# The seventh operand of a Strassen feed-forward, made before the stage instead of inside its first job

## The chip, the cores and the metric

The kernel runs on one core of one Trainium2 chip. The metric is the device time of one execution in microseconds (us), the median of several runs. Engines are named as the profile names them: PE (TensorE), PEld (its weight loads), DVE (VectorE), ACT (ScalarE), POOL (GpSimd) and SP (SyncE, which here only issues DMAs).

## What is computed

One layer of a hybrid encoder on 1024 positions of width 1024: a gated token mixer (a convolution module beside a bidirectional gated recurrence, the "scan"), its output projection, and a convolutional gated feed-forward with 2816 hidden columns. The part around the change is:

```python
x = x + jnp.einsum("bsd,de->bse", y, w_out[layer])
h2 = _rmsnorm(x, ffn_norm_w[layer])
up = jnp.einsum("bsd,df->bsf", h2, w_up)            # 1024 x 1024 times 1024 x 5632
gate, val = jnp.split(up, 2, axis=-1)
gate = _dwconv_centred(gate, dw_w, dw_b)            # three taps along the positions
x = x + jnp.einsum("bsf,fd->bsd", jax.nn.silu(gate) * val, w_down)
```

## The kernel before

**Layout.** Activations are held transposed, 128 channels by 512 positions a tile (2 KB in each partition), so 1024 x 1024 values are eight row groups by two halves. Every product is taken with split operands: `split` (L120) makes a high part by a cast on ACT (L121) and a low part by a subtraction on DVE (L118), and `mm3` (L138 to L145) issues three matmuls of 512 columns, high by high, high by low, low by high. The first of the three needs only the casts, the second the low part of the activations, the third the low part of the weights.

**The order.** PE executes its instructions in the order of the program text (L87). The other engines' queues are ordered by a planner, which walks the program with modelled durations before anything runs; on the chip each queue then executes in that fixed order, and an instruction that waits holds everything behind it on its engine.

**Memory pools.** A pool opened after another was released takes over its bytes. Its pages are held back one by one, each by the last use of the old pages that lie under it (`reuse_waits="tile"`). After the scan, its pool `hp` is released (L1058) and two are opened: `fw` (L1061), which lives to the end of the feed-forward's first half, and `p4` (L1062), which holds the merged activations `mg` and the tiles `x2` and `xq` for the output projection. After `p4.release()` (L1136), `fu` (L1139) takes over its bytes.

**The stages around the change.**
1. The last head of the scan and the last jobs of the projection `w_in` (`dense`), then the jobs with `hgrn_o_w` (L1083 to L1085). Their operand `bm` is loaded from DRAM into `tm` pages, split into `hx` pages (`bm_loads`, L1002), and merged with the gates by `merge` (L1065).
2. The jobs with `w_out` (L1118 to L1125). `x2_evac` (L1091) adds the input, stores `x2`, squares it for the norm and makes the scaled tile `xq`, stored as `d_h2` (`d_h` in the profile). After every second job the loop at L1126 to L1135 makes four operands of the next stage from the tiles still on the chip: numbers 1, 2, 6 and 5, each 4 row groups of a high and a low `hx` page.
3. The feed-forward's first half: 22 jobs `ffn_job(0..21)`, each a 2 x 2 block product by Strassen's scheme in Winograd's form, seven products (`pair_job`, L224) in the order 1, 2, 6, 7, 5, 4, 3, of 4 x 3 matmuls each. Below, "P7" is product 7, and "P7 of job 0" that of the first job.
4. `w_down` and the final norm.

**The weights of a job** (`prep`, L232): `rows` (a page of `wr`, two of them) and `col` (`sw`, a single page) are loaded by SP (L243, L244), `a22` (`w4`, a single page) too (L246). POOL issues three accumulating DMAs (`add`, L238): one adds to `col`, then one adds half of `col` to `rows`, then one adds the two halves of `rows`. Before, between and after these, five casts and subtractions make the split pages: w1 and w2 and later w6 and w3 in pages `wp` (four, in the pool `mp` that is always there); w7 and w5 from `col`, and w4 from `a22`, in pages `wq` (three). `wq`, `sw` and `w4` lie in the pool called `wpool`, which is `fw` for the feed-forward. A single `sw` page means that the next job's `col` is loaded when this job's w7 and w5 are split and its second `add` has landed. `run_jobs` (L149) prepares the next job four steps into the present one, that is after its second product.

**The operands 7, 4 and 3** are made from copies in DRAM after the first two products of job 0 have been issued (L1201 to L1219): `late_load` brings tiles back into `ft` pages (four of them, in `fu`). Operand 7 takes two loads, a subtraction (L1211) and a split for each of 4 row groups; operand 4 one load, two additions (L1216) and a split; operand 3 one load and a split. The results lie in 24 `hy` pages of `fu`. Between P1 and P2 stand 16 small matmuls for the norm (L420), and between P2 and P6 the matmuls that spread its result over the partitions (L412, fed by eight activations at L411).

Of the kernel before, what the change touches and what calls it, by code (L numbers as in the profile page):

```python
# [10 lines left out]
F32 = mybir.dt.float32  # L11
F32R = mybir.dt.float32r
# [3 lines left out]
ALU = mybir.AluOpType  # L16
AX = mybir.AxisListType

P = 128
# [25 lines left out]
def tile_hybrid_encoder(  # L45
# [24 lines left out]
    V, A, G, T = nc.vector, nc.scalar, nc.gpsimd, nc.tensor  # L70
# [20 lines left out]
    def nm(s):  # L91
        uid[0] += 1
        return f"{s}_{uid[0]}"
# [3 lines left out]
    def bank(tag):  # L97
        return ps.tile([P, H], F32, tag=tag, name=nm(tag), bufs=BANKS[tag])

    def page(pool, tag, bufs, dt=F32):  # L100
        return pool.tile([P, H], dt, tag=tag, name=nm(tag), bufs=bufs)

    def tmp():
        return page(mp, "tm", 4)
# [4 lines left out]
    def hx():  # L109
        return page(mp, "hx", 32, F32R)  # L110
# [6 lines left out]
    def split_lo(eng, lo, src, hi):  # L117
        eng.tensor_tensor(lo, src, hi.bitcast(F32), op=ALU.subtract)  # L118

    def split(hi, lo, src, eng):  # L120
        A.copy(hi, src)  # L121
        split_lo(eng, lo, src, hi)
        return hi, lo
# [4 lines left out]
    def raw_w(src, nk):  # L128
        t = mp.tile([P, nk, P], F32, tag="wr", name=nm("wr"), bufs=2)
        nc.sync.dma_start(t, src)  # L130
        return t

    def w_page(nk, pool=None):
        if pool is None:
            return mp.tile([P, nk, P], F32R, tag="wp", name=nm("wp"), bufs=4)
        return pool.tile([P, nk, P], F32R, tag="wq", name=nm("wq"), bufs=3)

    def mm3(acc, w, act, k, first, last, again=False):  # L138


        whi, wlo = w
        ahi, alo = act
        T.matmul(acc, whi[:, k, :], ahi, start=first, stop=False, skip_group_check=again)  # L143
        T.matmul(acc, whi[:, k, :], alo, start=False, stop=False, skip_group_check=again)  # L144
        T.matmul(acc, wlo[:, k, :], ahi, start=False, stop=last, skip_group_check=again)  # L145
# [78 lines left out]
    def pair_job(src0, src1, nk, acts, wpool, pool, evac, su=4):  # L224

        def prep():  # L232
            def both(src, alt):
                hi, lo = split(w_page(2 * nk, alt), w_page(2 * nk, alt), src, V)
                return [(hi[:, :nk], lo[:, :nk]), (hi[:, nk:], lo[:, nk:])]

            def add(o, a):
                G.dma_start(o, a, accum_op=ALU.add)  # L238

            w = {}  # L240
            rows = raw_w(src0, 2 * nk)
            col = wpool.tile([P, 2 * nk, P], F32, tag="sw", name=nm("sw"), bufs=1)
            nc.sync.dma_start(col[:, :nk], src0[:, :nk])  # L243
            nc.sync.dma_start(col[:, nk:], src1[:, :nk])  # L244
            a22 = wpool.tile([P, nk, P], F32, tag="w4", name=nm("w4"), bufs=1)
            nc.sync.dma_start(a22, src1[:, nk:])  # L246
            add(col, src1)
            w[1], w[2] = both(rows, None)
            add(rows[:, :nk], col[:, nk:])
            w[7], w[5] = both(col, wpool)  # L250
            add(rows[:, nk:], rows[:, :nk])
            w[6], w[3] = both(rows, None)
            one = w_page(2 * nk, wpool)
            w[4] = split(one[:, :nk], one[:, nk:], a22, V)
            return w

        def run(w):
            def product(i, acc, first=True):
                for k in range(nk):
                    mm3(acc, w[i], acts(i)[k], k, first and k == 0, k == nk - 1, not first)  # L260
                    if k % 2 == 1 or k == nk - 1:
                        yield

            def copy(acc):
                t = page(pool, "su", su)
                A.copy(t, acc)  # L266
                return t

            row, b2, col = bank("mm"), bank("tr"), bank("sc")
            yield from product(1, row)  # L270
            p1 = copy(row)
            yield from product(2, b2)
            evac(0, 0, b2, p1, ALU.add)
            yield from product(6, row, False)
            u2 = copy(row)
            yield from product(7, col)
            p7 = copy(col)
            yield from product(5, row, False)
            evac(1, 1, p7, row, ALU.subtract)
            yield from product(4, col, False)  # L280
            evac(1, 0, col, u2, ALU.subtract)
            yield from product(3, row, False)
            evac(0, 1, row)

        return prep, run

    def combos(ops, k, b11, b12, b22, alloc):
# [111 lines left out]
    NK2 = ND // 2  # L399
# [128 lines left out]
    for k in range(NK2):  # L528
        b21 = page(p1, "su", 4)
# [133 lines left out]
    for half in range(2):  # L663
        xs = []
        for j in range(NCW):
            if j % 2 == 0:
                both = p1.tile([P, 2, H], F32, tag="ca", name=nm("cx"), bufs=2)
# [16 lines left out]
        for j, xn in enumerate(xs):  # L684
# [3 lines left out]
            both = gp0.tile([P, 2, H], F32R, tag="gl", name=nm("ch"), bufs=NCW)  # L688
# [322 lines left out]
    for h in range(NH):  # L1011
# [4 lines left out]
        for half in range(2):  # L1016
            i = 2 * h + half
# [43 lines left out]
    fw = tc.alloc_tile_pool(name="fw", bufs=1, reuse_waits="tile")  # L1061
# [25 lines left out]
    h2 = {i: [] for i in range(1, 8)}  # L1087
# [23 lines left out]
        return evac  # L1111

    h2_pages = {i: [(hx(), hx()) for _ in range(NK2)] for i in (1, 2, 6, 5)}

    def parts(i, k, src):
        h2[i].append(split(*h2_pages[i][k], src, V))
# [9 lines left out]
    for k in range(NK2):  # L1126
        s_out.fill(16 if k else 17) if k < NK2 - 1 else s_out.drain()
        b11, b12, b21, b22 = x2[k][0], x2[k][1], x2[k + NK2][0], x2[k + NK2][1]
        t5, t6 = tmp(), tmp()
        parts(1, k, b11)  # L1130
        V.tensor_tensor(t5, b11, b12, op=ALU.subtract)
        parts(2, k, b21)
        V.scalar_tensor_tensor(t6, t5, -1.0, b22, op0=ALU.mult, op1=ALU.subtract)
        parts(6, k, t6)
        parts(5, k, t5)  # L1135
    p4.release()  # L1136

# [1 line left out]
    fu = tc.alloc_tile_pool(name="fu", bufs=1, reuse_waits="tile")  # L1139
# [59 lines left out]
    rstd2 = [next(st) for st in stats]  # L1199

    def late_parts(i, src):  # L1201
        h2[i].append(split(page(fu, "hy", 24, F32R), page(fu, "hy", 24, F32R), src, V))

    def late_load(kk, half):
        t = page(fu, "ft", 4)
        nc.sync.dma_start(t, d_h2[kk][half])
        return t

    for k in range(NK2):
        b12, b22 = late_load(k, 1), late_load(k + NK2, 1)  # L1210
        V.tensor_tensor(b12, b12, b22, op=ALU.subtract)  # L1211
        late_parts(7, b12)
    for k in range(NK2):
        b21 = late_load(k + NK2, 0)
        for part in h2[6][k]:
            V.tensor_tensor(b21, b21, part.bitcast(F32), op=ALU.add)  # L1216
        late_parts(4, b21)
    for k in range(NK2):
        late_parts(3, late_load(k + NK2, 1))  # L1219
# [152 lines left out]
```

## Time and profile before

| What | us |
|---|---|
| median of 3 runs | 1898.19 (1895.85 to 1900.01) |
| the profiled execution | 1905.6 |
| its span (first to last instruction) | 1903.8 |
| `w_out` jobs on PE, from 1099.8 to 1186.8 | 87.0 |
| first job of the feed-forward, from 1186.83 to 1226.18 | 39.35 |
| a later job, from 1245.80 to 1265.20 | 19.40 |

Times inside the execution are us from the start of the span. The profile's parts used below are its page (totals, the chain of work that ended last), the timeline of an engine (start, duration, engine, line, operation, out<-in, count, and in brackets the idle time before and what ended it), the busy time of the engines by stretches, groups of instructions, and DMA issues with their time to landing. "PEclk" is the share of its clock that PE was granted.

### The profile page before, as it was taken

To read this page: it belongs to the slowest core of one execution; us is meant where nothing else is said; L and a number is where in the kernel's file an instruction comes from. 1 tells how busy PE (TensorE), PEld (TensorE's weight loads), DVE (VectorE), ACT (ScalarE), POOL (GpSimd) and SP (SyncE) were. 2 spreads that over 40 slices of the span, in tenths; PEclk is the share of its full clock that TensorE was granted. 3 is DMA by queue.
4 is the path that set the end of the run, shared out by engine and by line. 5 is a ranking of instruction groups with operands and counts; after the bars stand their busy time and mean duration, and the time that the engine had idled before them with its cause. 6 is when DMAs were issued, how large, how long until landed. Compare 5 with 4: busy or idle time off the path is not lost.

```text
span 1903.8 us, 23750 instructions
## 1 busy us (share of the span) xinstructions
PE 1799.7 (95%) x8543; PEld 1484.0 (78%) x8543; DVE 1270.2 (67%) x1860; ACT 799.2 (42%) x1488; POOL 210.9 (11%) x218
## 2 busy tenths in 40 slices
PE   6988999999999998999998999899999999999996
PEld 5767878887778887888786888588888888788885
DVE  3488999535469898999835555667676666534445
ACT  6433333234554554555443134544343344522124
POOL 3101111213100001000100000111111111000000
PEclk9999999999999999999998999899999999999998
DMA  7747788786563333342237665777676676733134
GB/s 256 219 119 169 179 188 199 185 182 148 190 192 89 113 108 96 111 122 82 75 95 216 197 200 183 185 153 154 147 151 143 143 156 128 221 93 96 54 89 162
DMA packets 323916, 285.09 MB, mean 150 GB/s; under 512 B 14926, under 2 KB 245078, under 8 KB 323798
## 3 DMA queue, kind: packets, MB, share of 16 engines
q1 hardware_dynamic: 272006, 242.67, 41.5%
q0 software_dynamic: 51792, 40.90, 15.2%
q8 instruction: 67, 1.10, 0.3%
q14 instruction: 51, 0.42, 0.1%
HBM read 191.24 MB, written 71.83 MB: 138 GB/s over the span
## 4 chain that ended last, share of the span: by engine, by line
PE 66%; DVE 13%; DMA 8%; ACT 6%; issue 3%; POOL 2%; SPq 0%; ACTq 0%; POOLq 0%; DVEq 0%
PE mm L143 16%; PE mm L144 16%; PE mm L145 16%; PE sc L144 3%; PE sc L145 3%; PE sc L143 3%; PE tr L143 2%; PE tr L144 2%; PE tr L145 2%; DVE wp L118 1%; DVE kG L730 1%; DVE DE L730 1%; PE sc L838 1%; DVE qF L730 1%; DMA wr<-wr 1%
## 5 line engine op out<-in xcount | busy, mean ns | idle before, releaser
L143 PE MATMUL mm<-hx,wp 128*128 128x512 f32 x1176 | 482.6, 410 | 24.6 <-ACT hx L121 8.6
L145 PE MATMUL mm<-hx,wp 128*128 128x512 f32 x1176 | 467.4, 397 | 3.9 <-DVE wp L118 3.9
L144 PE MATMUL mm<-hx,wp 128*128 128x512 f32 x1176 | 466.8, 397 | 2.9 <-POOL hx L118 1.9
L121 ACT CAST wp<-wr 128x1024 fp32r<-128x1024 f32 (+2 forms) x196 | 179.7, 917 | 323.0 <-PE mm L144 222.9
L143 PEld LDWEIGHTS mm<-hx,wp 128*128 128x128 f32 x1176 | 226.5, 193 | 73.7 <-ACT hx L121 9.5
L118 DVE TENSOR_TENSOR wp<-wr,wp 128x1024 fp32r<-128x1024 f32 (+2 forms) x196 | 206.9, 1056 | 102.9 <-ACT wp L121 97.4
L145 PEld LDWEIGHTS mm<-hx,wp 128*128 128x128 f32 x1176 | 225.5, 192 | 55.1 <-DVE wp L118 5.4
L144 PEld LDWEIGHTS mm<-hx,wp 128*128 128x128 f32 x1176 | 226.5, 193 | 48.4 <-POOL hx L118 3.6
L645 DVE SCALAR_TENSOR_TENSOR acc<-gl,v_b,acc 128x1024 f32<-128x1024 f32 x120 | 150.1, 1285 | 0.5
L143 PE MATMUL sc<-hy,wq 128*128 128x512 f32 x244 | 97.3, 399 | 3.1 <-ACT hy L121 3.0
L144 PE MATMUL sc<-hy,wq 128*128 128x512 f32 x244 | 96.7, 396 | 2.7 <-DVE hy L118 2.7
L145 PE MATMUL sc<-hy,wq 128*128 128x512 f32 x244 | 96.2, 394 | 0.0
L238 POOL DMA_DIRECT2D wr<-sw x39 | 34.9, 896 | 519.3 <-DVE wp L118 297.4
L1251 DVE TENSOR_TENSOR xr<-mm,xr 128x512 f32<-128x512 f32 x48 | 33.1, 690 | 82.0 <-PE mm L145 82.0
L838 PEld LDWEIGHTS sc<-qF,A 128*128 128x128 f32 x512 | 65.9, 193 | 19.0 <-issue 13.3
L838 PE MATMUL sc<-qF,A 128*128 128x128 f32 x512 | 69.1, 278 | 11.7 <-DVE qF L730 10.6
L121 ACT CAST wq<-sw 128x1024 fp32r<-128x1024 f32 x39 | 41.1, 1054 | 86.6 <-PE mm L144 66.4
L143 PE MATMUL mm<-hy,wp 128*128 128x512 f32 x156 | 63.2, 405 | 7.4 <-ACT wp L121 5.3
L266 ACT COPY su<-mm 128x512 f32<-128x512 f32 x78 | 45.5, 583 | 53.4 <-PE mm L145 53.4
L835 ACT COPY A<-kG 128x512 f32<-128x512 f32 x64 | 39.7, 620 | 66.3 <-DVE kG L730 37.8
L1169 DVE SCALAR_TENSOR_TENSOR tm<-gp,v_a,tm 128x512 f32<-128x512 f32 x88 | 65.6, 746 | 1.8 <-ACT tm L1165 0.9
L1153 DVE TENSOR_TENSOR ft<-su,mm 128x512 f32<-128x512 f32 x22 | 15.1, 687 | 71.6 <-issue 68.1
(281 smaller groups left out, 3548.6 us busy)
## 6 DMA issues: line engine op xcount, KB each, us to landing
wr<-in_w_in_dram SPq DMA_DIRECT2D x55, 512.0 KB, 6.5
sw<-in_ffn_w_up_dram SPq DMA_DIRECT2D x44, 256.0 KB, 3.5
sw<-in_ffn_w_up_dram POOLq DMA_DIRECT2D x22, 512.0 KB, 8.3
wr<-in_ffn_w_up_dram SPq DMA_DIRECT2D x22, 512.0 KB
d_g<-ft SPq DMA_DIRECT2D x44, 256.0 KB, 5.9
ev<-d_g SPq DMA_DIRECT2D x44, 256.0 KB, 3.2
wr<-sw POOLq DMA_DIRECT2D x39, 256.0 KB, 3.3
wr<-wr POOLq DMA_DIRECT2D x39, 256.0 KB, 3.8
```

The source lines that it names most:

```text
L118: eng.tensor_tensor(lo, src, hi.bitcast(F32), op=ALU.subtract)
L121: A.copy(hi, src)
L143: T.matmul(acc, whi[:, k, :], ahi, start=first, stop=False, skip_group_check=again)
L144: T.matmul(acc, whi[:, k, :], alo, start=False, stop=False, skip_group_check=again)
L145: T.matmul(acc, wlo[:, k, :], ahi, start=False, stop=last, skip_group_check=again)
L238: G.dma_start(o, a, accum_op=ALU.add)
L266: A.copy(t, acc)
L645: V.scalar_tensor_tensor(acc, g[:, k : k + S], tap(k), acc, op0=ALU.mult, op1=ALU.add)
L730: V.tensor_tensor(o, a, b, op=op)
L835: A.copy(A_t.rearrange("p (b x e) -> p b x e", x=2, e=h), pairs(kG, h))
L838: T.matmul(b[:, c * P : (c + 1) * P].rearrange("p (b x e) -> p b x e", x=2, e=h), A_t[:, c * P : (c + 1) * P], view(qF, c * P, [[2 * h, P ...
L1169: V.scalar_tensor_tensor(c, g[:, o + k : o + k + H], vec("fdw", k * NF + j), c, op0=ALU.mult, op1=ALU.add,)
```

## The change

- Operand 7 is made in the loop at L1126 from the tiles still on the chip, with 1, 2, 6 and 5, into eight pages `h7` of a tag of its own in `fw`. Its difference t7 is taken first, t6 follows from t7 and t5 is taken last, so that the loop uses three temporary pages for each row group instead of two.
- The late loop for operand 7 (eight loads, four subtractions, four splits) is gone, and `hy` has 16 pages instead of 24.
- The pages `w4` and `wq` move from `wpool` to `pool`: for the feed-forward, from `fw` to `fu`. (For the jobs with `w_in`, which use the same function, both names mean one pool, and nothing moves.) `sw` stays in `fw`.

```diff
             col = wpool.tile([P, 2 * nk, P], F32, tag="sw", name=nm("sw"), bufs=1)
...
-            a22 = wpool.tile([P, nk, P], F32, tag="w4", name=nm("w4"), bufs=1)
+            a22 = pool.tile([P, nk, P], F32, tag="w4", name=nm("w4"), bufs=1)
...
-            w[7], w[5] = both(col, wpool)
+            w[7], w[5] = both(col, pool)
...
-            one = w_page(2 * nk, wpool)
+            one = w_page(2 * nk, pool)
...
     h2_pages = {i: [(hx(), hx()) for _ in range(NK2)] for i in (1, 2, 6, 5)}
+    h2_pages[7] = [[page(fw, "h7", 2 * NK2, F32R) for _ in range(2)] for _ in range(NK2)]
...
-        t5, t6 = tmp(), tmp()
+        t7, t6, t5 = tmp(), tmp(), tmp()
         parts(1, k, b11)
+        V.tensor_tensor(t7, b12, b22, op=ALU.subtract)
+        parts(2, k, b21)
+        V.tensor_tensor(t6, t7, b11, op=ALU.subtract)
+        parts(6, k, t6)
+        parts(7, k, t7)
         V.tensor_tensor(t5, b11, b12, op=ALU.subtract)
-        parts(2, k, b21)
-        V.scalar_tensor_tensor(t6, t5, -1.0, b22, op0=ALU.mult, op1=ALU.subtract)
-        parts(6, k, t6)
         parts(5, k, t5)
...
-        h2[i].append(split(page(fu, "hy", 24, F32R), page(fu, "hy", 24, F32R), src, V))
+        h2[i].append(split(page(fu, "hy", 16, F32R), page(fu, "hy", 16, F32R), src, V))
...
-    for k in range(NK2):
-        b12, b22 = late_load(k, 1), late_load(k + NK2, 1)
-        V.tensor_tensor(b12, b12, b22, op=ALU.subtract)
-        late_parts(7, b12)
```

## The prediction

> **What bounds the kernel now.** First the page: who is busy, and who stands on the chain that ended last.
>
> ```profile
> PE 1799.7 (95%) x8543; PEld 1484.0 (78%) x8543; DVE 1270.2 (67%) x1860; ACT 799.2 (42%) x1488; POOL 210.9 (11%) x218
> PE 66%; DVE 13%; DMA 8%; ACT 6%; issue 3%; POOL 2%; SPq 0%; ACTq 0%; POOLq 0%; DVEq 0%
> ```
>
> PE sets the time. A change that removes no matmul can gain only where PE stands still or runs slowly. So second, the busy times by stretches around the touched code:
>
> ```profile
> core 0: us, PE busy (x) PEld busy (x) DVE busy (x) ACT busy (x) POOL busy (x), PEclk, DMA share, GB/s
> 1002.57:1018.87 16.30, 7.04 (x17) 5.07 (x17) 8.15 (x12) 7.54 (x12) 0.00 (x0) 0.58 0.59 185
> 1199.40:1226.18 26.78, 19.83 (x50) 12.08 (x50) 19.94 (x30) 10.64 (x18) 3.40 (x3) 0.70 0.60 167
> 1245.80:1265.20 19.40, 19.40 (x86) 15.91 (x85) 12.69 (x17) 8.24 (x12) 3.33 (x3) 1.00 0.77 163
> 1099.80:1186.80 87.00, 87.00 (x385) 72.06 (x384) 45.41 (x63) 35.96 (x54) 1.73 (x2) 1.00 0.62 192
> ```
>
> In the `w_out` stage (last row) and in a later feed-forward job PE has no gap: nothing is to be had there, and work added there on DVE (45.41 of 87.00 us busy) is covered. 384 matmuls in 87.00 us give the full rate, 0.2266 us each. The two upper rows are the holes. The lower hole is where operands 7, 4 and 3 are made; PE's timeline:
>
> ```profile
> 1199.17 0.39 PE L145 MATMUL mm<-hx,wp 128*128 128x512 f32 x1
> ...
> 1200.05 0.49 PE L143 MATMUL sc<-hy,wq 128*128 128x512 f32 x1 [0.49 <-ACT hy L121]
> 1201.74 0.51 PE L144 MATMUL sc<-hy,wq 128*128 128x512 f32 x1 [1.20 <-DVE hy L118]
> ...
> 1220.92 0.76 PE L143 MATMUL mm<-hy,wp 128*128 128x512 f32 x1 [1.17 <-ACT hy L121]
> ...
> 1226.18 0.63 PE L143 MATMUL mm<-hx,wp 128*128 128x512 f32 x1
> ```
>
> P6 of job 0 ends at 1199.40 (one issue interval after the first row), job 1 begins at 1226.18. P7, P5, P4 and P3 are 48 matmuls, 10.9 us at the full rate, and take 26.78: **15.9 us too much**, in waits for `hy` and in matmuls at a clock of 0.70. What `hy` waits for, in the chain of work in order of time:
>
> ```profile
> 1192.66 6.56 DMA ft<-d_h
> ...
> 1201.72 3.08 DMA ft<-d_h
> ...
> 1205.61 3.24 DMA ft<-d_h
> ```
>
> It is the reloading of operand 7's tiles through four `ft` pages.
>
> The upper hole is at the end of the scan, 190 us ahead of the feed-forward. PE, then ACT, then the chain:
>
> ```profile
> 1002.34 0.39 PE L145 MATMUL mm<-hx,wp 128*128 128x512 f32 x1
> 1011.00 0.79 PE L143 MATMUL mm<-hx,wp 128*128 128x512 f32 x1 [8.27 <-ACT hx L121]
> 1012.79 0.80 PE L144 MATMUL mm<-hx,wp 128*128 128x512 f32 x1 [1.00 <-DVE hx L118]
> ```
>
> ```profile
> 998.05 0.62 ACT L121 CAST hx<-tm 128x512 fp32r<-128x512 f32 x1 [2.61 <-DMA tm<-d_bm]
> 998.92 0.63 ACT L121 CAST hx<-tm 128x512 fp32r<-128x512 f32 x1 [0.25 <-DMA tm<-d_bm]
> 1007.43 1.04 ACT L121 CAST wq<-sw 128x1024 fp32r<-128x1024 f32 x1 [7.88 <-DMA sw<-in_ffn_w_up_dram]
> 1008.39 0.61 ACT L121 CAST wq<-w 128x512 fp32r<-128x512 f32 x1
> 1008.91 1.04 ACT L121 CAST wp<-wr 128x1024 fp32r<-128x1024 f32 x1
> ...
> 1010.34 1.65 ACT L121 CAST hx<-tm 128x512 fp32r<-128x512 f32 x3
> ```
>
> ```profile
> 996.66 10.75 DMA sw<-in_ffn_w_up_dram
> ```
>
> PE waits for `bm`'s fifth row group. Its cast stands on ACT behind the casts of w7/w5 and w4 of feed-forward job 0, and these wait for the accumulating DMA into `sw`, which lands at 1007.41. The planner put them there because `wq` lies in `fw`, which opens after the scan. From 1002.57 to 1018.87 PE issues 15 matmuls, 3.4 us at the full rate: **12.9 us too much**.
>
> **The change part by part.** *wq and w4 to `fu`.* Their pages now lie under `mg`, which is read to the end of `w_out`. So the two casts and two subtractions cannot stand at 1007 any more, nor the `a22` loads at SP's head:
>
> ```profile
> 993.97 0.92 SPq L114 DMA_DIRECT2D tm<-d_bm  x2
> ...
> 999.42 2.05 SPq L114 DMA_DIRECT2D tm<-d_bm  x3
> 1010.37 0.38 SPq L246 DMA_DIRECT2D w<-in_ffn_w_up_dram  x1
> ```
>
> What is late next is `bm` itself. The two loads issued from 993.97 released casts at 998.05 and 998.92, some 4.2 us each; the three issued from 999.42 share the engines with the accumulate, so I take landings of 1005, 1006 and 1007 (bounds: 1003.6 by 4.2 us, 1007.4 when the accumulate is over). A cast (0.62) and PE resumes at 1005.7; the last group's low part is there at 1008.6, and the four groups are through at about 1009.9 instead of 1005.3: 4.6 us stay. Before, the clock was 0.58 in that stretch, and 12.9 less the two waits of PE (8.27 and 1.00) leaves 3.6 us to it. A gap of 3.1 us may do it too: 0 to 4 us, I take 2. So 6.6 of 12.9 stay, **6.3 gained** (3 to 8.3).
> The Trainium skill ("TensorE: Matmul & The Clock Gate", section "What's actually happening") says that the clock halves after an idle window of about 3.4 us and returns after a busy one, and that the windows run freely; it speaks against a full gain, since 3.1 us is under it by little. By it alone the term would be 0 or about 1.7 us (half of 3.4, an estimate); the trace agrees that the clock is halved after 8.27 us, and no row shows a gap of 3.1.
>
> *Operand 7 from tiles on the chip.* Gone: eight loads of 256 KB, four subtractions at L1211, four casts and four low parts. Added in the loop: for each row group one subtraction (t7), one cast, one low part. Prices:
>
> ```profile
> L118 DVE TENSOR_TENSOR hy<-ft,hy 128x512 fp32r<-128x512 f32 x12 | 8.1, 687 | 1.9 <-ACT hy L121 1.8
> L1216 DVE TENSOR_TENSOR ft<-ft,hx 128x512 f32<-128x512 f32 x8 | 5.2, 686 | 1.3 <-DMA ft<-d_h 1.3
> L1211 DVE TENSOR_TENSOR ft<-ft,ft 128x512 f32<-128x512 f32 x4 | 2.8, 690 | 5.3 <-DMA ft<-d_h 5.3
> ```
>
> That is 1.4 us of DVE and 0.62 of ACT a row group. Three of the four lie under `w_out`, where DVE has 41 us to spare; without that cover they would cost 4. The third `tm` page delays nothing there: a job takes PE 10.9 us. The fourth group comes after `w_out`, with the casts that moved (1.05 and 0.62 on ACT, 1.22 and 0.69 on DVE). Behind them stand the norm's activations, for which P6 waits; ACT and DVE have gaps there, so I take 0.7 (0 to 5: the rival below).
>
> Then P7 and P5 follow P6 at once, and P4 is wanted at 1204.8, P3 at 1207.6. DVE can begin the eight additions and four low parts of operand 4 when the first four late loads land, 1198 as before, and needs 8.2 us for them (0.69 each) and some 1.7 for what stands between: P4 is late by 0 to 2, I take 0.5. Operand 3 gets its `ft` pages one by one from operand 4, each load 3.1 us (second and third row of the chain above), a cast and a low part: its last group stands at about 1212, wanted at 1209.9, 2.2 us.
>
> Last, the weights of job 1. `sw` is reloaded when w7/w5 of job 0 are split, now at about 1192.5 instead of 1182:
>
> ```profile
> 1188.00 1.57 POOL L238 DMA_DIRECT2D sw<-in_ffn_w_up_dram  x1 [4.95 <-DMA sw<-in_ffn_w_up_dram]
> ...
> 1201.38 0.95 POOL L238 DMA_DIRECT2D wr<-sw  x1 [7.75 <-DVE wp L118]
> 1206.37 0.87 POOL L238 DMA_DIRECT2D wr<-wr  x1 [4.04 <-DMA wr<-sw]
> ```
>
> ```profile
> sw<-in_ffn_w_up_dram POOLq DMA_DIRECT2D x2, 512.0 KB, 7.7
> ...
> sw<-in_ffn_w_up_dram SPq DMA_DIRECT2D x2, 256.0 KB, 4.3
> ...
> wr<-sw POOLq DMA_DIRECT2D x1, 256.0 KB, 4.7
> wr<-wr POOLq DMA_DIRECT2D x1, 256.0 KB, 4.8
> ```
>
> 4.3 + 7.7 + 4.7 + 4.8 us, a cast of 1.05 and 1 for issues make 23.6: w6 of job 1 stands at 1216, wanted by its P6 at 1212.5 + 5.4 = 1218. It fits by 2 us; I take 1 (0 to 5) for what the loads do to each other, and 1 (0 to 4) for a clock that falls in these waits. Later jobs have the cover of the gapless row above. Together 5.4 of 15.9 stay, **10.5 gained** (5 to 14.4).
> The Trainium skill ("DMA: Bandwidth & Descriptors", section "Issuing engines are not separate DMA queues") says that DMAs from all queues interleave on the same 16 engines, which speaks against moving `a22` and `sw` to 1190; it names no price, and by it the 1 us becomes the 5 of my range.
>
> **The sum.** 6.3 + 10.5 = 16.8 us off the span of 1903.8: 1887.0. The profiled execution (1905.6) is 7.4 above the median, so the difference is taken from the median: 1898.19 - 16.8 = **1881.4**.
>
> **The rivals.**
> - *Only the feed-forward gains.* `bm` lands late anyway, or another cast with a wait takes the head of ACT at 1000. For: the accumulate still runs there. Against: `bm`'s casts at 1010.34 waited for no DMA. 1898.2 - 10.5 = 1887.7.
> - *Only the scan's end gains.* `a22` is loaded at 1190, lands after 6.6 us as `ft` did, and its cast on ACT holds the norm's activations: P6 5 us later, and 3.6 us of slow clock as at the scan's end. The second gain falls to 10.5 - 8.6 = 1.9: 1898.2 - 8.2 = 1890.0.
> - *Slower: the reload of `sw`.* If SP has it behind the late loads, as job 2's reload was before (row below), it goes out at about 1217, w6 of job 1 stands at 1240.6, and PE waits 22.6 us from 1218 and loses 3.6 to the clock: 4.4 + 22.6 + 3.6 = 30.6 instead of the 15.9 lost there before, less the 6.3 gained: 8.4 us slower, 1906.6. Each us of the reload is one of the time; it decides from 1208.5. Against: eight late loads are half of sixteen, and the planner let a ready `sw` load go first at 1181.97.
>
> ```profile
> 1181.97 0.38 SPq L243 DMA_DIRECT2D sw<-in_ffn_w_up_dram  x1
> ...
> 1218.40 0.38 SPq L243 DMA_DIRECT2D sw<-in_ffn_w_up_dram  x1
> ```
>
> - *It does nothing:* the planner, which orders everything anew, makes waits elsewhere (at the end of the feed-forward's first half, say) that eat the gain: 1898.
>
> **Chances.** Forecast 0.60 (gains of 3 + 5 to 8.3 + 14.4: 1875.5 to 1890), feed-forward only 0.12, scan only 0.11, slower 0.09, nothing 0.08. Range 1874 to 1893: it leaves out the last two and the edges of the others. A measurement of this kernel tells about 0.2%, 3.8 us. Faster 0.83, same 0.08, slower 0.09.
>
> **What would show it.** No `wq` cast near 1007, and a gap of PE there of 2 to 4 us. No L1211; P7 right behind P6; gaps at P4 and P3 under 3 us; the reload of `sw` before 1195 and no wait of PE for `wp` in job 1. Wrong would be a gap of over 5 us between P2 and P6, a `sw` reload after 1205, or a hole that stays at 1002 to 1011.

## The result, and the profile after

The median after is 1890.92 us (9 runs, 1886.05 to 1897.06); before, on the same chip, 1900.52 us (9 runs). The ratio is 0.9955 (95% interval 0.9938 to 0.9972): 8.6 us faster (5.3 to 11.8), where 16.8 were forecast. The time, 1890.92, lies inside the forecast's range and 9.5 us above its point. Three more comparisons of the same kernel gave 0.9947, 0.9939 and 0.9950 (intervals with the experiments); over all of them the medians are 1890.4 us (39 runs) and 1900.7 us (87 runs), so the gain is some 10 us.

The profiled execution of after took 1889.98 us, with a span of 1888.2. From its page, totals by engine: PE has the same 8543 instructions as before and is busy 9.3 us less; most of that is in P7 to P3, where its busy time fell from 19.83 to 11.10 us and PEclk rose from 0.70 to 1.00.

```profile
PE 1790.4 (95%) x8543; PEld 1477.7 (78%) x8543; DVE 1270.7 (67%) x1860; ACT 797.8 (42%) x1488; POOL 212.4 (11%) x218
```

Now the stretches, cut at the same matmuls in each kernel. Busy time of the engines, PEclk, DMA share and GB/s, first two stretches of before that the prediction did not show (from the last four matmuls of P2 to the end of P6 of job 0, called "P2 to P6" below; job 1), then four of after (the scan's end; P2 to P6; P7 to P3; job 1):

```profile
1193.20:1199.40 6.20, 5.93 (x21) 3.42 (x19) 2.04 (x4) 4.46 (x12) 0.44 (x5) 1.00 1.03 288
1226.18:1245.80 19.62, 19.62 (x85) 16.05 (x84) 12.87 (x17) 9.32 (x12) 1.75 (x2) 0.98 0.72 160
```

```profile
1001.07:1008.96 7.89, 5.73 (x17) 3.74 (x16) 3.37 (x5) 2.99 (x5) 0.00 (x0) 0.78 1.14 324
1184.67:1196.28 11.61, 8.52 (x22) 4.96 (x21) 8.62 (x13) 7.69 (x17) 2.84 (x3) 0.71 0.58 177
1196.28:1207.38 11.10, 11.10 (x49) 9.02 (x48) 9.64 (x14) 6.67 (x11) 1.76 (x2) 1.00 0.80 168
1207.38:1228.66 21.28, 19.59 (x86) 15.70 (x85) 12.96 (x17) 9.28 (x12) 3.34 (x3) 1.00 0.73 160
```

The scan's end fell from 16.30 to 7.89 us, and P7 to P3 from 26.78 to 11.10, which is the full rate of 10.9. Two stretches grew: P2 to P6 from 6.20 to 11.61, and job 1 from 19.62 to 21.28. PE's timeline at the scan's end of after, then the cast on ACT that it waits for:

```profile
1000.84 0.39 PE L145 MATMUL mm<-hx,wp 128*128 128x512 f32 x1
1003.16 0.50 PE L143 MATMUL mm<-hx,wp 128*128 128x512 f32 x1 [1.94 <-ACT hx L121]
1003.89 0.78 PE L144 MATMUL mm<-hx,wp 128*128 128x512 f32 x1 [0.23 <-DVE hx L118]
```

```profile
1002.49 0.62 ACT L121 CAST hx<-tm 128x512 fp32r<-128x512 f32 x1 [3.12 <-DMA tm<-d_bm]
```

The wait of 8.27 us is one of 1.94. The `wq` cast is gone from there, and the cast of `bm` waits for its own load alone. PE and then ACT where the norm is spread over the partitions (L411 to L413), in after:

```profile
1185.36 0.39 PE L145 MATMUL tr<-hx,wp 128*128 128x512 f32 x1
1187.58 1.44 PE L412 MATMUL sc<-tm,ones_m 128*128 128x512 f32 x2 [1.83 <-ACT tm L411]
1190.28 2.08 PE L412 MATMUL sc<-tm,ones_m 128*128 128x512 f32 x2 [1.27 <-ACT tm L411]
1191.37 1.42 PE L143 MATMUL mm<-hx,wp 128*128 128x512 f32 x1
1192.58 0.63 PE L144 MATMUL mm<-hx,wp 128*128 128x512 f32 x1
1193.01 0.63 PE L145 MATMUL mm<-hx,wp 128*128 128x512 f32 x1
...
1196.27 0.40 PE L143 MATMUL sc<-h,wq 128*128 128x512 f32 x1
```

```profile
1184.30 0.99 ACT L411 ACTIVATE tm<-ident,r 128x128 f32<-128x128 f32 x3 [0.88 <-POOL r L405]
1185.19 0.60 ACT L121 CAST hx<-tm 128x512 fp32r<-128x512 f32 x1
1185.70 1.04 ACT L121 CAST wq<-sw 128x1024 fp32r<-128x1024 f32 x1
1186.65 0.58 ACT L266 COPY su<-mm 128x512 f32<-128x512 f32 x1
1187.12 0.69 ACT L411 ACTIVATE tm<-ident,r 128x128 f32<-128x128 f32 x2
1187.72 0.61 ACT L121 CAST wq<-w 128x512 fp32r<-128x512 f32 x1
1188.23 0.40 ACT L411 ACTIVATE tm<-ident,r 128x128 f32<-128x128 f32 x1
1189.05 0.59 ACT L413 COPY rs<-sc 128x512 f32<-128x512 f32 x1 [0.42 <-PE sc L412]
1189.54 0.69 ACT L411 ACTIVATE tm<-ident,r 128x128 f32<-128x128 f32 x2
```

ACT has no gap to speak of between the first scaling and the sixth. The scalings are the activations at L411. Between the third and the fourth stand a cast of the last row group, the moved `wq` cast and an eviction (the copy of P1's result out of its bank, `su`, L266, without which P6 can't begin, since it adds into that bank). PE waits 1.83 us for that fourth scaling. It waits 1.27 us for the second half, and then runs the next matmuls at 0.43 us each instead of 0.2266.

### The profile page after: what moved, and what is told of

Its sections match the earlier page's. It is cut to its first block, busy times and chain, and to the rows that moved or that the text cites. A ratio compares the mean times of both kernels' runs of the same rounds, so it can differ in the third digit from the quotient of the medians.

```text
span 1888.2 us, 23731 instructions
## 1 busy us (share of the span) xinstructions
PE 1790.4 (95%) x8543; PEld 1477.7 (78%) x8543; DVE 1270.7 (67%) x1860; ACT 797.8 (42%) x1488; POOL 212.4 (11%) x218
## 3 DMA queue, kind: packets, MB, share of 16 engines
q0 software_dynamic: 51792, 40.90, 15.3%
## 5 line engine op out<-in xcount | busy, mean ns | idle before, releaser
L838 PE MATMUL sc<-qF,A 128*128 128x128 f32 x512 | 68.2, 276 | 11.7 <-DVE qF L730 10.6
L143 PE MATMUL mm<-hy,wp 128*128 128x512 f32 x156 | 62.2, 399 | 8.9 <-ACT wp L121 5.9
L266 ACT COPY su<-mm 128x512 f32<-128x512 f32 x78 | 45.4, 581 | 48.7 <-PE mm L145 48.5
L144 PE MATMUL mm<-hy,wp 128*128 128x512 f32 x156 | 61.8, 396 | 0.0
L145 PE MATMUL mm<-hy,wp 128*128 128x512 f32 x156 | 61.3, 393 | 0.0
L143 PE MATMUL tr<-hx,wp 128*128 128x512 f32 x156 | 61.2, 392 | 0.0
L143 PE MATMUL sc<-hy,wq 128*128 128x512 f32 x156 | 61.1, 392 | 0.0
```

The costliest lines, as they stand in the source:

```text
L838: T.matmul(b[:, c * P : (c + 1) * P].rearrange("p (b x e) -> p b x e", x=2, e=h), A_t[:, c * P : (c + 1) * P], view(qF, c * P, [[2 * h, P ...
```

## The experiments

Fourteen runs were made. The table gives, for each profiled execution, the four stretches in us, by the starts of PE's matmuls (A: the scan's end, B: P2 to P6, C: P7 to P3, D: job 1), and the ratio of the timed runs to before, with its interval. Line numbers shift by a few where lines were added. The recorded expectations cut some stretches elsewhere than the table, and what they call a "partition" of a job is one product or a few: the last one, which waits for the norm, is P6, and the third or seventh is P3.

| Kernel | A | B | C | D | ratio to before |
|---|---|---|---|---|---|
| before, three profiles | 16.3, 15.3, 15.4 | 6.2, 6.2, 6.2 | 26.8, 25.5, 26.6 | 19.6, 19.2, 19.3 | 1 |
| after (first) | 7.9 | 11.6 | 11.1 | 21.3 | 0.9955 (0.9938 to 0.9972) |
| a1 (after) | 8.5 | 11.6 | 11.1 | 25.9 | 0.9947 (0.9931 to 0.9963) |
| a2 (after) | 7.9 | 11.8 | 11.1 | 21.1 | 0.9939 (0.9925 to 0.9953) |
| a3 (after) | 9.5 | 10.7 | 11.1 | 25.9 | 0.9950 (0.9928 to 0.9972) |
| wq_only | 8.1 | 7.7 | 25.9 | 19.5 | 0.9974 (0.9959 to 0.9989) |
| norm_first | 8.2 | 10.3 | 20.0 | 19.3 | 0.9962 (0.9948 to 0.9976) |
| sw_two | 8.3 | 10.6 | 12.0 | 21.8 | 0.9945 (0.9927 to 0.9963) |
| both | 9.5 | 10.2 | 17.2 | 19.3 | 0.9936 (0.9919 to 0.9953) |
| add_pool | 7.7 | 10.6 | 12.4 | 19.3 | 0.9930 (0.9905 to 0.9956) |
| add_pool2 (the same) | 8.1 | 10.6 | 12.0 | 19.3 | 0.9927 (0.9901 to 0.9953) |
| spread_split | 8.3 | 12.8 | 12.1 | 19.4 | 0.9948 (0.9929 to 0.9967) |
| add_split | 8.6 | 12.7 | 13.7 | 19.3 | 0.9945 (0.9926 to 0.9963) |
| ord2 | 8.7 | 6.2 | 24.2 | 19.3 | 0.9962 (0.9942 to 0.9983) |

**b1 and b2: before again.**

> The kernel before, unchanged, for a second profile of it. Theory (the profile shown of before was one of the longer executions: 1905.6 us against a median of 1900.5): a profile near 1900 us, with the same two holes (12.9 us at the end of the scan, 15.9 us in the first job of the feed-forward) within 1 us each, and the rest of the difference in stages that the change does not touch. Rival (the holes themselves vary with the landing times of the transfers): one of the holes is shorter by 3 us or more.

> The kernel before, a third profile. Theory (the stages that the change does not touch wander by a few us from execution to execution, and the two profiles so far were late by 2 to 4 us at 950 us): the time up to the end of the scan lies 2 to 4 us lower than in the two, and the two holes keep their size within 1 us (20 us for the stretch with the scan's end, 22 us for that of the feed-forward). Rival (the holes themselves are smaller in most executions, and the traces of before are unlike its timed runs): one of the two stretches is shorter by 3 us or more.

They took 1906.4 and 1904.8 us in their profiled executions, so b1 was not near 1900 as expected, and all three profiles of before lie above its timed median. The holes keep their size within 1.4 us in all three profiles (table; 1 us was expected), so the rival, holes that vary by 3 us or more, falls. Stages that no edit here touches wander more. Busy times of a stretch in the scan, cut at the same matmuls, in before and in b1:

```profile
890.86:909.56 18.70, 15.95 (x102) 13.52 (x100) 15.44 (x28) 10.77 (x28) 1.53 (x2) 1.00 0.44 141
```

```profile
888.68:911.91 23.23, 18.87 (x101) 15.77 (x100) 14.77 (x27) 14.02 (x34) 1.80 (x2) 0.85 0.34 113
```

18.70 against 23.23 us with the same code; b1's PE waited 3.48 us once for ACT there and lost its clock. So two profiles may be compared stretch by stretch, but not by their totals. b2 came to the hole at 1000.65 us, 1.9 and 4.5 us ahead of the other two, where 2 to 4 were expected.

**a1, a2, a3: after again.**

> The kernel after, unchanged, for a second profile and a closer ratio. Theory: 9 to 10 us faster than before (ratio 0.995), and in its profile the norm of the first feed-forward job again loses 5 us between the first and the last of its spread, and the second job's first partition 1 to 2 us. Rival (the two losses were one execution's accident): 13 to 16 us faster, and the norm loses under 2 us.

> The kernel after once more, beside the three edits on the same chip: 9 to 11 us faster than before, ratio 0.994 to 0.9955, and again a loss of 5 us in the norm of job 0 and of 1 to 5 us ahead of job 1's last partition.

> The kernel after, a fourth profile, beside the two edits below on the same chip. Theory (the forecast's gain was too large by the norm's 5.4 us and by a wait of 2 to 7 us for the weights of job 1, both there in each profile so far): again 11.1 to 11.3 us for the stretch of the norm, against 5.7 before, again 5.9 us or more for the first partition of job 1, against 4.1, and 9 to 11 us faster than before in the timed runs. Rival (the wait for the weights of job 1 is there only in some executions): 4.1 us for that partition.

B is 10.7 to 11.8 in all four profiles of after: the norm's loss is no accident, though in a3 it was a us less than expected. D is 21.1 to 21.3 in two and 25.9 in two, a loss of some 2 us and of over 6; for a1, one of the latter, 1 to 2 were expected. The chain of work in a1, in order of time, tells what D waits for:

```profile
1205.61 7.02 DMA wr<-wr
1212.70 1.04 ACT wp L121
1213.75 0.72 ACT tm L1168
1214.48 1.28 ACT L1180
1215.78 0.63 ACT tm L1180
1216.41 0.48 ACT su L266
1216.93 0.80 PE mm L143
```

The cast that waits, in a1, and PE's wait in after and in a1:

```profile
1212.70 1.04 ACT L121 CAST wp<-wr 128x1024 fp32r<-128x1024 f32 x1 [7.44 <-DMA wr<-wr]
```

```profile
1214.69 0.50 PE L143 MATMUL mm<-hx,wp 128*128 128x512 f32 x1 [1.70 <-ACT su L266]
```

```profile
1216.93 0.80 PE L143 MATMUL mm<-hx,wp 128*128 128x512 f32 x1 [4.17 <-ACT su L266]
```

In a1 the cast of `wp` for w6 of job 1 stands at ACT's head from 1205 and waits 7.44 us for the third accumulating transfer. Behind it stand two activations of job 0, a load of an activation table (L1180, 1.28 us), and then the eviction `su` (L266) that frees PE's bank. PE waits 4.17 us for that eviction. In the first profile of after the same transfer landed sooner, and the wait was 1.70. The four profiles go together in this: the transfer took 5.1 and 5.0 us in after and a2, where D is 21.3 and 21.1, and 7.0 and 7.1 in a1 and a3, where D is 25.9. Why it took longer in two of them is not shown. DMA issues of the two profiles, KB and us from issue to landing (after, then a1):

```profile
wr<-wr POOLq DMA_DIRECT2D x1, 256.0 KB, 5.1
```

```profile
wr<-wr POOLq DMA_DIRECT2D x1, 256.0 KB, 7.0
```

**wq_only: the moved pages alone.**

```diff
-            a22 = wpool.tile([P, nk, P], F32, tag="w4", name=nm("w4"), bufs=1)
+            a22 = pool.tile([P, nk, P], F32, tag="w4", name=nm("w4"), bufs=1)
...
-            w[7], w[5] = both(col, wpool)
+            w[7], w[5] = both(col, pool)
...
-            one = w_page(2 * nk, wpool)
+            one = w_page(2 * nk, pool)
```

> Before with the late weight pages of the scan's side moved to the later pool and nothing else; the feed-forward's seventh operand is still made late. Theory: the hole at the end of the scan falls by 6 to 8 us and the hole of the feed-forward stays at 14 to 17 us, so 4 to 8 us faster than before (ratio 0.996 to 0.998). Rival (all of the gain is the feed-forward's): within 2 us of before. Second rival (the moved pages pay nothing, since the activations of the norm wait for the casts in their place): the scan's hole shrinks and the first feed-forward job's norm loses 5 us, within 2 us of before.

The busy times of its scan's end and of P7 to P3:

```profile
995.87:1003.99 8.12, 5.47 (x17) 3.84 (x16) 3.37 (x5) 3.00 (x5) 0.00 (x0) 0.79 1.11 315
1187.27:1213.20 25.93, 17.74 (x50) 11.60 (x49) 16.92 (x26) 8.75 (x16) 4.34 (x4) 0.75 0.74 180
```

The theory holds: A falls as in after, C stays. The two holes are separate, each closed by its own part of the change. 5 us faster (2 to 8), with B 1.5 us longer: that much of the norm's loss comes with the moved casts alone. The rest is left, by subtraction, to what operand 7 adds behind the last `xq`; operand 7 alone was not run.

**norm_first: the norm's steps ahead of the casts** (`tc.high_priority()` has the planner put what stands under it first).

```diff
-    for st in stats:
-        next(st)
+    with tc.high_priority():
+        for st in stats:
+            next(st)
     s_ffn.fill(2)
-    rstd2 = [next(st) for st in stats]
+    with tc.high_priority():
+        rstd2 = [next(st) for st in stats]
```

> The kernel after with the feed-forward norm's own steps put ahead of the casts on ScalarE and VectorE; nothing else moved. Theory (between the two column sums and the last partition of job 0, TensorE waits on the norm's eight scalings, which stand behind a cast of a part, an eviction and two weight casts): TensorE reaches that partition 3 to 5 us sooner than after, so 3 to 5 us faster than after (ratio to before 0.992 to 0.993). Rival (the loss is the throttled clock and not the order): the two waits at the spread stay at 1 us or more each, within 1 us of after. Second rival (the casts that now stand behind the norm are late for the next partitions): the norm is shorter, and the seventh partition or the second job waits as much longer.

PE's waits in job 0, from its timeline:

```profile
1187.40 1.12 PE L412 MATMUL sc<-tm,ones_m 128*128 128x512 f32 x2 [0.42 <-ACT tm L411]
1190.82 0.67 PE L143 MATMUL mm<-hx,wp 128*128 128x512 f32 x1 [2.29 <-ACT su L266]
1210.31 0.77 PE L143 MATMUL mm<-hy,wp 128*128 128x512 f32 x1 [6.52 <-DVE ft L1156]
```

The waits at the spread fell from 3.1 to 0.42 us, so they were ACT's and DVE's order. But the eviction that P6 needs now stands behind the casts, and P3 waits 6.52 us: the second rival. The kernel is no faster than after. D is at its full rate there, 19.3 us, without any edit to the weights. B and C together take 30.3 us there, against 22.7 in after, so the weights of job 1 seem to have had the time.

**sw_two: a second page for the folded columns** (`pair_job` gets `odd`, true for odd jobs).

```diff
-            col = wpool.tile([P, 2 * nk, P], F32, tag="sw", name=nm("sw"), bufs=1)
+            where, tag = (pool, "sx") if odd else (wpool, "sw")
+            col = where.tile([P, 2 * nk, P], F32, tag=tag, name=nm(tag), bufs=1)
```

> The kernel after with a second page for the folded columns, taken by the odd feed-forward jobs; nothing else moved. Theory (jobs 1 to 3 start late because the one page is read by job 0's cast until 1187, and two accumulating transfers of 8 and 4 us follow it): the waits ahead of the last partition of jobs 1 to 3 go, 2 to 5 us faster than after (ratio to before 0.992 to 0.994). Rival (these waits are the transfers' own, queued behind the late loads): the chain ends no sooner, within 1 us of after, the same gap of 1 to 2 us in job 1.

D is 21.8, so the theory falls. The POOL timeline, accumulating transfers of jobs 1 and 2:

```profile
1195.25 1.63 POOL L238 DMA_DIRECT2D sx<-in_ffn_w_up_dram  x1 [5.54 <-ACT wp L121]
1198.54 1.57 POOL L238 DMA_DIRECT2D sw<-in_ffn_w_up_dram  x1 [1.67 <-DVE hy L118]
1203.32 0.90 POOL L238 DMA_DIRECT2D wr<-sx  x1 [3.21 <-ACT hy L121]
1209.56 0.87 POOL L238 DMA_DIRECT2D wr<-wr  x1 [5.35 <-DMA wr<-sx]
```

Job 2's transfer into the free page went ahead of job 1's second and third, and the third is issued 21.2 us after the start of stretch B, against 20.7 in after. So a second page alone brought nothing. What it would bring if job 1's transfers went first, this run does not show.

**both: norm_first and sw_two together.**

> The two edits together. Theory (two separate losses): their gains add, 5 to 9 us faster than after, near 1883 us (ratio to before 0.990 to 0.992). Rival (they are in series: a norm that ends sooner only makes the second job wait longer for its weights): little more than the larger of the two alone.

P3 still waits 4.16 us where norm_first had 6.52. D is at its full rate, 19.3, but so it was in norm_first alone, so that is not the second page's doing. The ratio is that of after within its interval: the gains do not add. That speaks for the rival, losses in series, though what waits longer is P3 of job 0 and not job 1.

**add_pool and add_pool2: the second and third sum of the weights of jobs 1 to 3 on GpSimd** (`near` is true for these jobs).

```diff
+            def add_sb(o, a):
+                if near:
+                    G.tensor_tensor(o, o, a, op=ALU.add)
+                else:
+                    add(o, a)
...
-            add(rows[:, :nk], col[:, nk:])
+            add_sb(rows[:, :nk], col[:, nk:])
...
-            add(rows[:, nk:], rows[:, :nk])
+            add_sb(rows[:, nk:], rows[:, :nk])
```

> The kernel after with the second and the third sum of the weights of the feed-forward's jobs 1 to 3 made on GpSimd as two additions of 128x512 instead of two accumulating transfers; nothing else moved. Theory (the weight cast of job 1 stands at the head of ScalarE's queue until the third accumulating transfer has landed, near 1210 to 1213 us, and the evictions stand behind it): the two additions take 3 to 4 us (1.45 to 1.59 us each in the rows of another line) where the two transfers took 9 to 11, the cast runs 5 to 8 us sooner, TensorE's wait on the eviction in job 1 (1.7 and 4.2 us in two profiles of after) goes, and the kernel is 2 to 4 us faster than after (ratio to before 0.993). Rival (TensorE waits for the first transfer into the shared page): the wait stays above 1 us, within 1 us of after.

> The kernel after with the second and third sum of the weights of jobs 1 to 3 on GpSimd, for a closer ratio beside after on the same chip. Theory: the first partition of job 1 again takes 4.1 us, and the kernel is 2 to 4 us faster than after (ratio to before lower by 0.001 to 0.002). Rival (what is gained there is lost to the wander of other stages, or to GpSimd's additions beside VectorE's work): the same as after within 1 us.

POOL's timeline and the busy times of job 1, in add_pool2:

```profile
1197.81 1.51 POOL L242 TENSOR_TENSOR wr<-wr,sw 128x512 f32<-128x512 f32 x1 [6.03 <-DMA ft<-d_h]
1199.40 1.64 POOL L242 TENSOR_TENSOR wr<-wr 128x512 f32<-128x512 f32 x1
```

```profile
1204.62:1223.90 19.28, 19.28 (x85) 15.79 (x84) 13.35 (x18) 9.62 (x12) 4.17 (x3) 1.00 0.72 177
```

Two additions of 3.2 us stand where two transfers took 9 to 11, and D is 19.3 in both profiles instead of 21.1 to 25.9. Job 1 had no more time for it than in after: B and C together take 23.0 and 22.6 us, and 22.7 in the first profile of after. That settles the place of the loss. Its price in timed runs is open: beside after (a3) on the same chip the ratios are 0.9927 and 0.9950, a lead of some 4 us, but the intervals overlap. Its two ratios are the lowest of all kernels here.

**spread_split and add_split: the second half's four scalings on GpSimd** (`pool` is true for that half), **and this together with add_pool.**

```diff
+            if pool:
+                G.tensor_scalar(
+                    diag[:, c * P : (c + 1) * P], ident, r[:, c : c + 1], None, op0=ALU.mult
+                )
+                continue
             A.activation(diag[:, c * P : (c + 1) * P], ident, AF.Copy, scale=r[:, c : c + 1])
```

> The kernel after with the four scalings of the norm's second half made on GpSimd instead of ScalarE; nothing else moved. Theory (ScalarE has some 7 us of work between the column sums and the last partition of job 0, in a stretch of 5 us): 1.2 us of it go, TensorE's second wait at the spread (1.27 us) goes and job 0's last partition starts 1 to 3 us sooner; 1 to 3 us faster than after. Rival (what is gained at the spread is lost behind it, as when the norm was put first: the evictions or the late parts then end last): the spread is shorter, the third partition of job 0 waits as much longer, within 1 us of after. Second rival (GpSimd's scalings are slow): the second wait grows above 2 us.

> The two edits together. Theory (two separate losses, each taken where it arises, without a cast or an eviction put behind another): the gains add, 3 to 7 us faster than after, near 1884 us where after has 1890 (ratio to before 0.990 to 0.9925). Rival (they share a queue, GpSimd's, and the first addition stands behind the scalings): no more than the larger of the two.

The second rival: the four scalings took POOL 4.75 us, some 1.2 each, where ACT takes 0.3 to 0.4. B grew to 12.8, and job 1, which begins later by that, has D at 19.4. In D and its ratio the pair is no better than add_pool, so its theory, gains that add, falls. POOL in spread_split:

```profile
1192.39 4.75 POOL L412 TENSOR_SCALAR tm<-ident,r 128x128 f32<-128x128 f32 x4
```

**ord2: add_pool, norm_first, and job 0's first eviction and late parts at high priority too** (`soon` is true for job 0).

```diff
+            if soon:
+                with tc.high_priority():
+                    p1 = copy(row)
+            else:
+                p1 = copy(row)
...
+        with tc.high_priority():
+            h2[i].append(split(page(fu, "hy", 16, F32R), page(fu, "hy", 16, F32R), src, V))
```

> The sums of jobs 1 to 3 on GpSimd, the norm's steps ahead of the casts, and job 0's first eviction ahead of them too, so that its last partition has neither to wait for. Theory of the series (the norm and the chain that starts from the weight cast of job 0, over the reload of the shared page and the first accumulating transfer, to the late parts and the evictions behind job 1's cast on ScalarE, want the same engine at the same time): the last partition of job 0 starts 2 to 4 us sooner than in after, its third partition waits 4 to 8 us, and the total is within 2 us of the kernel with the sums alone. Rival (only the eviction was missing when the norm was put first): the third partition waits under 2 us and 3 to 6 us are gained over the kernel with the sums alone.

The busy times of B and C, then PE's longest wait and ACT ahead of it:

```profile
1189.03:1195.27 6.24, 5.92 (x21) 3.60 (x20) 4.59 (x8) 6.19 (x14) 1.20 (x5) 1.00 0.53 191
1195.27:1219.51 24.24, 13.25 (x49) 10.09 (x48) 15.66 (x22) 8.08 (x14) 6.60 (x4) 0.79 0.61 138
```

```profile
1215.07 0.77 PE L143 MATMUL mm<-hy,wp 128*128 128x512 f32 x1 [10.72 <-DVE ft L1166]
```

```profile
1208.94 1.05 ACT L121 CAST wq<-sw 128x1024 fp32r<-128x1024 f32 x1 [7.06 <-DMA sw<-in_ffn_w_up_dram]
1209.89 0.61 ACT L121 CAST hy<-ft 128x512 fp32r<-128x512 f32 x1
...
1210.93 1.66 ACT L121 CAST hy<-ft 128x512 fp32r<-128x512 f32 x3
```

B is back at before's 6.2 us, so the norm's whole loss is order and clock. C is 24.2. With the norm first, the planner put job 1's `wq` cast ahead of four of the late `hy` casts on ACT, where in after only one stands behind it; it waits 7.06 us for the first accumulating transfer, and DVE's subtractions and the eviction at L1166 wait with it. The wait is longer than the 4 to 8 us expected, and the median is 7.6 us above add_pool2's (1894.13 against 1886.57), where at most 2 were expected. The chain runs from the `wq` cast of job 0 over the reload of `sw`, the accumulating transfer and the `wq` cast of job 1 to the late parts; with the norm first, the `wq` cast of job 0 began 3.5 us after the start of B instead of 1.0, the reload followed at 6.2 instead of 3.4, and PE came to P7 5.4 us sooner. So the loss at the norm, as it stands in after, covers a chain that ends later when the norm is put first. Whether some order has both short is open; none of those run here has.

## Why the prediction was wrong in size

- **The scan's end: right.** The step left 6.6 of 12.9 us: 4.6 of waiting and pace and 2 of clock. After keeps 4.5 in the first profile (7.89 less 3.4), 2.2 in waits and 2.3 in clock, and 4.5 to 6.1 over the four. Against three profiles of before the mean gain is 7.2 us, where 6.3 were forecast. The accumulating transfer still ran there, as the first rival had it, but no cast waited for it. Whether it slowed `bm`'s load, which took 5.54 us where the one before took 3.37, is not shown. wq_only shows that the moved pages did it.
- **P7 to P3: right in kind, too careful.** The steps for P4 and P3 left 2.7 us; 0.2 stayed. The first four late loads went out at 1182.16, ahead of the end of P2, and the loss at the norm gave the rest 5 us. So a part of this gain is owed to the step that failed, and is no merit of the estimate: in ord2 and norm_first, with the norm first, C is 24.2 and 20.0.
- **The norm: the failed step.** "ACT and DVE have gaps there, so I take 0.7", with 0 to 5 as its bounds. It measured 5.2 us on the mean (11.4 against 6.2): 3.1 in two waits, and some 2 in the clock, for which the term had nothing. The gaps were before's. In after the casts that moved, the cast of the last row group, two halves of the norm and an eviction fall into the same 6 us of ACT, in an order that the planner chose. The waits alone lie within the bounds; with the clock the loss passes their top. One of the prediction's own signs of being wrong came with it, a gap of over 5 us between P2 and P6 (from 1185.59 to 1191.37, with the spread's four matmuls in it). This is the place of the second rival, but not its mechanism: `a22`'s cast, at 1187.72, waited for nothing. It was work in the way, not a late transfer. norm_first and ord2 show it by taking the waits away.
- **The weights of job 1: the second failed step.** It compared when w6 stands with when P6 wants it: "it fits by 2 us; I take 1". The sum for the chain was right: from the reload at 1188.03 it took 23.5 us in after, where 23.6 were forecast, and the cast ended at 1211.5, before PE came to P6 near 1213. But PE waited for the eviction behind the cast, which the step had left out: 1.7 us in one profile, and 4.17 in another, where the cast itself ended only at 1213.7, with some 2.4 more of clock. D is 4.2 us longer on the mean (23.5 against 19.4), where the step and its clock had 2. add_pool shows the chain's part by shortening it.
- **The reload of `sw`** went out at 1188.03, well ahead of 1208.5; the slower rival had no ground.
- **The sum.** By the four stretches the mean is 67.5 us in three profiles of before and 54.5 in four of after: 13.0 gained (7.2 - 5.2 + 15.2 - 4.2), where 16.8 were forecast. Timed, it is some 10. The other 3 us are not settled. The four profiles of after differ by 5 us among themselves in these stretches, and the profiled executions of before (1905.6, 1906.4, 1904.8) all lie above the median of 1900.7, while those of after average 1890.4, which is their median. The prediction took its base from the median and its gain from such an execution, and had no term for that. Its sum also had a small slip: by its own times job 1 begins at 1212.5, only 2.2 us after the full rate allows (1199.4 plus 10.9), so the 0.7 and 0.5 lie inside that wait and were counted twice. Without them it would have forecast 1.2 us more.

## What to carry to other kernels

A transfer that is waited for costs what stands behind the waiting instruction on its engine, not only what consumes it: follow the queue to the eviction. Gaps of an engine read in the trace of before are no room for moved work when the change also pulls the consumers together. Where an in-order queue is filled by a planner, an edit that shortens one wait may let a cast that waits for a transfer go ahead of others; look at the order, not only at the edited lines.

## What the runs showed of the hardware

- Gaps of about 2 us can halve PE's clock. After 1.94 us of waiting and 0.23 more at the scan's end, eight matmuls came at 0.42 us or slower; nearly the same after 2.71 us in a1 and 2.59 in wq_only. After 1.70 us in job 1 the rate stayed at 0.23. In the first profile of after PEclk is 0.50 from 1003.94 to 1007.35 and from 1188.26 to 1195.09; in the 3.41 us before each fall PE was busy for 1.25 and 1.58 us. In the 3.42 us up to 1215.57, which hold the gap of job 1, it was busy for 1.73, and PEclk stayed at 1.00. So the work around a gap seems to count too; three stretches give no threshold. The Trainium skill ("TensorE: Matmul & The Clock Gate", section "What's actually happening") gives an idle window of about 3.4 us for it; by that alone the gap of 1.94 would have cost no clock, and the measurement decides: it cost 2.3 us.
- The same accumulating transfer of 256 KB took 5.0 to 5.1 us in two executions and 7.0 to 7.1 in two, and with it job 1 lost 2 or 6 us.
- GpSimd took 1.2 us to scale a 128x128 tile by a value per partition (four in 4.75 us, where ACT took 0.99 for three), and 1.3 to 1.7 to add two of 128x512 in add_pool and add_pool2.
